# Score matmuls of two or four heads tied together in one two-bank PSUM tile, in a two-layer hybrid decoder trunk

## The chip, the cores and the metric

The kernel runs on one core of one Trainium2 chip. The metric is the device time of one execution in microseconds (us), the median of several runs. The engines are PE (TensorE: matmuls, with PEld for the loading of their stationary operands), DVE (VectorE), ACT (ScalarE), POOL (GpSimd) and SP, which issues most DMAs. PSUM, where matmuls write, has eight banks of 512 fp32 columns.

## The reference, cut to what matters

Two layers over 512 positions of width 1024, in fp32. Layer 0 (mLSTM and pooling) is untouched by the change. Layer 1 is a sparse attention with 16 heads of 64 columns and an indexer of 4 heads of 64 columns that picks keys:

```python
score = jnp.einsum('bqh,bqhs->bqs', wib, jax.nn.relu(jnp.einsum('bqhd,bsd->bqhs', qib, ki)))
score = jnp.where((key_pos[None, :] <= t[:, None])[None], score, -jnp.inf)
_, idx = lax.top_k(score, top_k)
...
logits = jnp.einsum('bqhd,bqkhd->bqhk', qb, ksel).astype(jnp.float32) * (C_HEAD_DIM ** -0.5)
logits = logits + bias.transpose(0, 1, 3, 2)
logits = jnp.where(valid[:, :, None, :], logits, -jnp.inf)
probs = jax.nn.softmax(logits, axis=-1).astype(v.dtype)
return jnp.einsum('bqhk,bqkhd->bqhd', probs, vsel)
```

## The kernel before, in words

Every fp32 operand is split into a high and a low half, and each product is three matmuls (high by high, high by low, low by high).

Layer 1 works in blocks of 128 queries (i = 0 to 3), with n = 128 (i + 1) keys, and in four groups c of four heads. `scores(i)` (called for i = 1, 2, 3) makes the indexer's scores, `select(i, part)` marks the largest of them by rounds of MAX8 and MATCH_REPLACE on DVE, and `attend(c, i)` does one block of queries for four heads, two pairs of heads one after the other. A pair is: score matmuls into PSUM (`qk`), bias and mask added on the way out of PSUM by DVE (L808, which also gives the row's extreme), exp on ACT (L810), reciprocal on DVE (L811), scaling on ACT (L812), transposes on PE (L820, into `tr`), their split on ACT and DVE (`pt_h`, `pt_l`), nine or so matmuls with the values (L829 to L831, into `po`), and a product with the gate on DVE (L835). The bias tile `cb` that L808 reads is made by POOL (L805) in one of two buffers.

A head has 64 columns, so a score matmul contracts over 64 rows only. Two heads of a pair lie in rows 0 to 63 and 64 to 127 of the same tiles. `head_pair` writes its six matmuls (three products of two heads) in turn, e = 0 and e = 1, into two separate banks:

```python
p = [bank("qk"), bank("qk")]
for j in range(3):
    for e in range(2):
```

`qk` is a pool of two buffers of one bank each, so a pair takes both, and each bank is free for the next pair once its own head has been read out. The projections around (`q_proj`, `k_proj`, `v_proj`, `z_proj`, `ckv_proj`; matmuls at L182 to L184 and L198 to L200 into `mm`) run over all this time and fill PE between the steps of the attention.

`ORDER` gives the order in which the steps are written, but the order on each engine is made when the kernel is built: a list scheduler takes the instructions by their priority as soon as, by its own reckoning, their inputs and buffers are free. So the six matmuls of a pair need not stand side by side on PE. There are 228 score matmuls, all at L669: 108 over 256 columns (keys), 60 over 384 and 60 over 512.

The last step, the output projection, uses `dense_ch4` twice (hf = 0, 1): four accumulators each, two from `mm` and two from `qk`, read out by `store` (L848).

Of the kernel before, what the change touches and what calls it, by code (L numbers as in the profile page):

```python
# [2 lines left out]

# [5 lines left out]
F32 = mybir.dt.float32  # L9
# [49 lines left out]
def trunk(ctx: ExitStack, tc: tile.TileContext, a: dict, out: bass.AP):  # L59
    nc = tc.nc  # L60
    V, A, G, T = nc.vector, nc.scalar, nc.gpsimd, nc.tensor
# [5 lines left out]
    ps = {}  # L67
    ps_pools = ExitStack()

    def psum_pools(**banks):  # L70
        ps_pools.close()
        ps.clear()
        for n, b in banks.items():
            ps[n] = ps_pools.enter_context(tc.tile_pool(name="ps_" + n, bufs=b, space=PSUM))
# [4 lines left out]
    def bank(n):  # L79
        return ps[n].tile([128, 512], F32, name=n)  # L80

    def mm():
        return bank("mm")
# [31 lines left out]
    def split(h, l, src):  # L115
        A.copy(h, src)  # L116
        sub_f32r(l, src, h)
# [17 lines left out]
    def wtile(shape, loads, queue=nc.sync):  # L135
        n = math.prod(shape)
        raw = wp.tile([128, 1024], F32, name="raw", bufs=3)
        wh = wp.tile([128, 1024], F32R, name="wh")
        wl = wp.tile([128, 1024], F32R, name="wl")

        def view(t):
            t = t[:, :n]
            if len(shape) == 2:
                t = t.rearrange("p (x y) -> p x y", x=shape[0])
            return t
        for sl, src in loads:
            queue.dma_start(view(raw)[:, sl[0], sl[1]], src)
        A.copy(wh[:, :n], raw[:, :n])  # L148
        low_engine[0].tensor_tensor(wl[:, :n], raw[:, :n], wh[:, :n].bitcast(F32), op=ALU.subtract)  # L149
        return view(wh), view(wl)  # L150
# [3 lines left out]
    def wrows(w, r0, nk, c0, n):  # L154
        return w[r0:r0 + 128 * nk, c0:c0 + n].rearrange("(k p) c -> p k c", p=128)
# [38 lines left out]
    def part_ch(act, w, ks, ps):  # L194
        wh, wl = w
        for j, k in enumerate(ks):
            ah, al = act(k)
            T.matmul(ps, wh[:, j], ah, start=(k == 0), stop=False)  # L198
            T.matmul(ps, wh[:, j], al, start=False, stop=False)  # L199
            T.matmul(ps, wl[:, j], ah, start=False, stop=(k == NK - 1))  # L200

    def dense_ch4(act, w, hf, evac, alloc):

        acc = [alloc(c) for c in range(4)]
        for k0 in range(0, NK, 2):
            wh, wl = wtile([2, 512], [((ALL, ALL), wrows(w, 128 * k0, 2, 512 * hf, 512))])
            for c in range(4):
                cs = slice(128 * c, 128 * c + 128)
                part_ch(act, (wh[:, :, cs], wl[:, :, cs]), (k0, k0 + 1), acc[c])
                if k0 == NK - 2:  # L210
                    evac(4 * hf + c, acc[c])
# [8 lines left out]
    xn = lambda k: (xn_h[:, k], xn_l[:, k])  # L220
# [105 lines left out]
    w_in, w_out = a["e_w_in"], a["e_w_out"]  # L326


    with ExitStack() as l0:
# [141 lines left out]
        with ExitStack() as la:  # L471
            p0 = la.enter_context(tc.tile_pool(name="p0a", bufs=1))
# [134 lines left out]

    w_in, w_out = a["o_w_in"], a["o_w_out"]
    w_uk, w_uv = a["o_w_uk"], a["o_w_uv"]
    psum_pools(mm=2, bg=1, qk=2, tr=2, po=1)  # L610
    GR = ((0, 1), (2, 3))
    p2 = ctx.enter_context(tc.tile_pool(name="p2", bufs=1))
    zy = p2.tile([128, 8, S], F32, name="zy")
# [8 lines left out]
    qi_h, qi_l = (p1.tile([128, 2, S], F32R, name=n, tag=n, bufs=2) for n in ("aq_h", "aq_l"))  # L622
    ki_h, ki_l = (p2.tile([128, S], F32R, name=n, tag=n, bufs=3) for n in ("ak_h", "ak_l"))
# [36 lines left out]
    def ckv_proj():  # L660
        dense_tok(xn, range(NK), [(w_in, 1024, 256)], ev_ckv, GR)

    def head_pair(q, k, n):

        p = [bank("qk"), bank("qk")]
        for j in range(3):
            for e in range(2):
                es = slice(64 * e, 64 * e + 64)
                T.matmul(p[e][:, :n], q(es, j), k(es, j), start=(j == 0), stop=(j == 2))  # L669
        return p  # L670

    near = {0: tmask}
    far = {}
# [2 lines left out]
    def scores(i):  # L676
        n = 128 * (i + 1)
        qs = slice(128 * i, 128 * i + 128)
        acc = sel[i] = (p2 if i == 3 else p1).tile([128, n], F32, name=f"sel{i}")
        G.memset(acc[:, :n - 128], 0.0)  # L680
        G.tensor_copy(acc[:, n - 128:], tmask)
        pair = {}
        for h in range(4):
            if h % 2 == 0:
                pair = head_pair(lambda e, j: (qi_h, qi_h, qi_l)[j][e, h // 2, qs],
                                 lambda e, j: (ki_h, ki_l, ki_h)[j][e, :n], n)
            p = pair[h % 2]
            rl = t1.tile([128, 512], F32, name="relu", tag="cb")
            A.activation(rl[:, :n], p[:, :n], AF.Relu)
            V.scalar_tensor_tensor(acc, rl[:, :n], wi[:, i, h:h + 1], acc, op0=ALU.mult, op1=ALU.add)  # L690
# [93 lines left out]
    def attend(c, i):  # L784
        (q_h, q_l), (k_h, k_l), (v_h, v_l) = Q[c]["q"], Q[c]["k"], Q[c]["v"]
        bias = Q[c]["bias"]
        n = 128 * (i + 1)
        nn = max(n, 256)
        qs = slice(128 * i, 128 * i + 128)
        lo = max(n - 256, 0)  # L790
        for pr in range(2):
            probs = []
            pq = head_pair(lambda e, j: (q_h, q_h, q_l)[j][e, pr, qs], lambda e, j: (k_h, k_l, k_h)[j][e, pr, :nn], nn)
            for e in range(2):
                hd = 2 * pr + e
                p = pq[e]
                if i == 3:
                    cb = sel[i][e]
                else:
                    cb = t1.tile([128, 384], F32, name="cb", tag="cb")  # L800
                    if lo:
                        G.tensor_copy(cb[:, :lo], far[i])
                rev = bias[:, hd, n - lo - 1:n - lo]
                rev = bass.AP(tensor=rev.tensor, offset=rev.offset, ap=[rev.ap[0], [-1, n - lo]])
                G.tensor_tensor(cb[:, lo:n], near[i], rev, op=ALU.add)  # L805
                lg = p2.tile([128, 512], F32, name="lg", tag="lg", bufs=6)
                st = t1.tile([128, 4], F32, name="st", bufs=4)
                V.tensor_tensor_reduce(out=lg[:, :n], in0=p[:, :n], in1=cb[:, :n], scale=-1.0, scalar=3e38,  # L808
                                       op0=ALU.add, op1=ALU.min, accum_out=st[:, 0:1])
                A.activation(lg[:, :n], lg[:, :n], AF.Exp, scale=-1.0, bias=st[:, 0:1], accum_out=st[:, 1:2])  # L810
                V.reciprocal(st[:, 2:3], st[:, 1:2])  # L811
                A.activation(lg[:, :n], lg[:, :n], AF.Copy, scale=st[:, 2:3])  # L812
                probs.append(lg)
            po = bank("po")
            for s0 in range(0, i + 1, 2):
                ss = range(s0, min(s0 + 2, i + 1))
                p = bank("tr")
                for s in ss:
                    for e in range(2):
                        T.transpose(p[:, 256 * (s - s0) + 128 * e:256 * (s - s0) + 128 * e + 128],  # L820
                                    probs[e][:, 128 * s:128 * s + 128], ident)
                m = 256 * len(ss)
                pt_h = p2.tile([128, 512], F32R, name="pt_h", bufs=2)
                pt_l = p2.tile([128, 512], F32R, name="pt_l", bufs=2)
                split(pt_h[:, :m], pt_l[:, :m], p[:, :m])
                for s in ss:
                    cs = slice(128 * pr, 128 * pr + 128)
                    ps = slice(256 * (s - s0), 256 * (s - s0) + 256)
                    T.matmul(po[:, :256], v_h[:, s, cs], pt_h[:, ps], start=(s == 0), stop=False)  # L829
                    T.matmul(po[:, :256], v_l[:, s, cs], pt_h[:, ps], start=False, stop=False)  # L830
                    T.matmul(po[:, :256], v_h[:, s, cs], pt_l[:, ps], start=False, stop=(s == i))  # L831
            for e in range(2):
                es = slice(64 * e, 64 * e + 64)
                y = zy[es, 2 * c + pr, qs]
                V.tensor_tensor(y, po[es, 128 * e:128 * e + 128], y, op=ALU.mult)  # L835

    def y_split(c, i=None):

        cs, qs = slice(2 * c, 2 * c + 2), ALL if i is None else slice(128 * i, 128 * i + 128)
        split(xn_h[:, cs, qs], xn_l[:, cs, qs], zy[:, cs, qs])  # L840

    step = dict(i=scores, c=ckv_proj, q=q_proj, k=k_proj, v=v_proj, z=z_proj, s=select, a=attend, y=y_split)
    run(ORDER, **step)

# [4 lines left out]
        nc.scalar.dma_start(out[128 * c:128 * c + 128], o)  # L849

    for hf in range(2):
        dense_ch4(xn, w_out, hf, store, lambda c: bank(("mm", "qk", "mm", "qk")[c]))


def layout(inputs):
# [34 lines left out]
```

## Time and profile before

| | us |
|---|---|
| three runs, median (lowest to highest) | 774.74 (774.5 to 776.12) |
| the profiled execution, device time | 773.58 |
| its span, first to last instruction | 771.8 |
| PE busy in the span | 751.6 (97%) |
| DVE busy | 464.8 (60%) |
| ACT busy | 398.1 (52%) |
| POOL busy | 304.7 (39%) |
| score matmuls (L669), first to last start | 488.8 to 723.8 |

The profiled execution took 1.8 us more than its span, and lies 1.2 us under the median. Busy time of PE is counted from overlapping matmuls (each starts before the one ahead has drained), so it says that PE had something in it, not that it worked at its peak. What a matmul costs the stream is read from one start to the next.

### The profile page before, as it was taken

Reading aid. Unit: us, or ns where it says so; the run is one execution under the profiler, and the core shown is the slowest. Engines: PE = TensorE matmul, PEld = TensorE weight load, DVE = VectorE, ACT = ScalarE, POOL = GpSimd, SP = SyncE. Lnnn points to the kernel's source line nnn. Section 1 sums busy time; section 2 is a strip of 40 time slices with the busy share of each in tenths; the row PEclk is TensorE's granted clock in tenths of the full one; section 3 lists DMA queues with packets and bytes.
Section 4 is the critical chain, followed back from the end, with each engine's and each line's share of the span. In section 5 each row is a group of like instructions: output and inputs, shape, how many; then the busy total and the mean of one; then the engine's idle time right before and its main releaser. Section 6 shows DMA issues by size and latency. Waiting matters only on the chain.

```text
span 771.8 us, 11177 instructions
## 1 busy us (share of the span) xinstructions
PE 751.6 (97%) x4123; PEld 631.6 (82%) x4123; DVE 464.8 (60%) x988; ACT 398.1 (52%) x778; POOL 304.7 (39%) x246
## 2 busy tenths in 40 slices
PE   7989999999999999999999999998999999999988
PEld 5887888887888889888888888987788888887766
DVE  6686534344727765147224572599999978877531
ACT  6445333282445543355433353545667688887620
POOL 5545448732003020131363393445124555472241
PEclk9999999999999999999999999999999999999999
DMA  7523342345332313332322244422321221020051
GB/s 222 155 75 84 84 108 74 105 122 150 106 86 69 87 63 110 82 96 87 89 84 61 88 154 123 111 69 69 82 69 42 69 69 55 9 91 13 28 192 54
DMA packets 83990, 69.20 MB, mean 90 GB/s; under 512 B 3884, under 2 KB 71900, under 8 KB 83936
## 3 DMA queue, kind: packets, MB, share of 16 engines
q1 hardware_dynamic: 82144, 65.83, 29.6%
q10 hardware_dynamic: 1760, 2.66, 1.0%
q8 instruction: 32, 0.52, 0.3%
q14 instruction: 22, 0.18, 0.1%
q0 software_dynamic: 32, 0.01, 0.0%
HBM read 64.25 MB, written 4.23 MB: 89 GB/s over the span
## 4 chain that ended last, share of the span: by engine, by line
PE 84%; DVE 9%; ACT 2%; DMA 2%; issue 2%; POOL 1%; SPq 1%; DVEq 0%; ACTq 0%; POOLq 0%
PE mm L198 13%; PE mm L199 13%; PE mm L200 12%; PE mm L182 8%; PE mm L183 8%; PE mm L184 8%; PE qk L669 5%; PE tr L820 2%; PE po L829 2%; PE po L831 2%; DVE sel L698 1%; DVE m L697 1%; DMA raw<-in_e_w_in_dram 1%; PE po L830 1%; DVE wl L149 1%
## 5 line engine op out<-in xcount | busy, mean ns | idle before, releaser
L149 POOL TENSOR_TENSOR wl<-raw,wh 128x1024 fp32r<-128x1024 f32 (+4 forms) x65 | 148.7, 2290 | 274.4 <-ACT wh L148 230.6
L148 ACT CAST wh<-raw 128x1024 fp32r<-128x1024 f32 (+4 forms) x117 | 113.4, 971 | 172.8 <-PE mm L199 52.3
L198 PE MATMUL mm<-xn_h,wh 128*128 128x512 f32 x336 | 132.8, 397 | 3.1 <-DVE v_l L363 2.0
L200 PE MATMUL mm<-xn_h,wl 128*128 128x512 f32 x336 | 132.6, 395 | 0.0
L199 PE MATMUL mm<-xn_l,wh 128*128 128x512 f32 x336 | 132.3, 394 | 0.0
L183 PE MATMUL mm<-wl,xn_h 128*128 128x256 f32 (+2 forms) x384 | 123.9, 323 | 0.0
L184 PE MATMUL mm<-wh,xn_l 128*128 128x256 f32 (+2 forms) x384 | 123.2, 322 | 0.0
L182 PE MATMUL mm<-wh,xn_h 128*128 128x256 f32 (+2 forms) x384 | 121.6, 325 | 1.0 <-DVE xT L595 0.9
L149 DVE TENSOR_TENSOR wl<-raw,wh 128x1024 fp32r<-128x1024 f32 (+2 forms) x52 | 66.0, 1269 | 63.2 <-ACT wh L148 62.7
L182 PEld LDWEIGHTS mm<-wh,xn_h 128*128 128x128 f32 x384 | 72.0, 189 | 9.2 <-ACT wh L148 1.3
L183 PEld LDWEIGHTS mm<-wl,xn_h 128*128 128x128 f32 x384 | 72.3, 188 | 7.0 <-issue 1.1
L184 PEld LDWEIGHTS mm<-wh,xn_l 128*128 128x128 f32 x384 | 72.2, 188 | 6.7 <-issue 0.7
L198 PEld LDWEIGHTS mm<-xn_h,wh 128*128 128x128 f32 x336 | 63.2, 189 | 17.1 <-DVE v_l L363 2.1
L199 PEld LDWEIGHTS mm<-xn_l,wh 128*128 128x128 f32 x336 | 63.3, 188 | 14.5 <-issue 0.6
L200 PEld LDWEIGHTS mm<-xn_h,wl 128*128 128x128 f32 x336 | 63.3, 188 | 13.8
L200 PE MATMUL mm<-y_h,wl 128*128 128x512 f32 x128 | 50.1, 393 | 0.6 <-DVE wl L149 0.6
L199 PE MATMUL mm<-y_l,wh 128*128 128x512 f32 x128 | 50.4, 394 | 0.0
L198 PE MATMUL mm<-y_h,wh 128*128 128x512 f32 x128 | 48.9, 395 | 0.9 <-ACT y_h L116 0.9
L504 DVE SCALAR_TENSOR_TENSOR cv<-mm,s_conv,cv 128x511 f32<-128x511 f32 (+2 forms) x48 | 35.9, 747 | 16.3 <-ACT cv L502 15.3
L810 ACT ACTIVATE lg<-lg,st 128x128 f32<-128x128 f32 (+3 forms) x64 | 35.8, 561 | 6.1 <-DVE st L808 5.9
L812 ACT ACTIVATE lg<-lg,st 128x128 f32<-128x128 f32 (+3 forms) x64 | 34.0, 557 | 7.4 <-DVE st L811 7.4
L805 POOL TENSOR_TENSOR cb<-sel,abias 128x256 f32<-128x256 f32 x32 | 24.5, 770 | 30.1 <-DVE st L808 22.1
(272 smaller groups left out, 1578.0 us busy)
## 6 DMA issues: line engine op xcount, KB each, us to landing
raw<-in_e_w_in_dram SPq DMA_DIRECT2D x52, 512.0 KB, 3.8
raw<-in_o_w_in_dram SPq DMA_DIRECT2D x18, 512.0 KB, 3.9
raw<-in_e_w_out_dram SPq DMA_DIRECT2D x16, 512.0 KB, 3.8
raw<-in_o_w_out_dram SPq DMA_DIRECT2D x8, 512.0 KB, 3.6
xT<-in_xT_dram SPq DMA_DIRECT2D x8, 256.0 KB, 4.2
x_one<-xT SPq DMA_DIRECT2D x8, 256.0 KB, 3.0
abias<-lines SPq DMA_DIRECT2D x4, 512.0 KB, 4.2
o_sb<-x_one SPq DMA_DIRECT2D x8, 256.0 KB, 4.4
```

What stands on the lines that cost most here:

```text
L148: A.copy(wh[:, :n], raw[:, :n])
L149: low_engine[0].tensor_tensor(wl[:, :n], raw[:, :n], wh[:, :n].bitcast(F32), op=ALU.subtract)
L182: T.matmul(acc[t][:, :n], ah[:, ts], wh[:, j], start=first, stop=False)
L183: T.matmul(acc[t][:, :n], ah[:, ts], wl[:, j], start=False, stop=False)
L184: T.matmul(acc[t][:, :n], al[:, ts], wh[:, j], start=False, stop=last)
L198: T.matmul(ps, wh[:, j], ah, start=(k == 0), stop=False)
L199: T.matmul(ps, wh[:, j], al, start=False, stop=False)
L200: T.matmul(ps, wl[:, j], ah, start=False, stop=(k == NK - 1))
L504: V.scalar_tensor_tensor(u[:, j:], ps[:, :S - j], w[:, 3 - j:4 - j], u[:, j:], op0=ALU.mult, op1=ALU.add)
L669: T.matmul(p[e][:, :n], q(es, j), k(es, j), start=(j == 0), stop=(j == 2))
L810: A.activation(lg[:, :n], lg[:, :n], AF.Exp, scale=-1.0, bias=st[:, 0:1], accum_out=st[:, 1:2])
L812: A.activation(lg[:, :n], lg[:, :n], AF.Copy, scale=st[:, 2:3])
```

## The change

`head_pairs` takes one tile of two banks from `qk`, whose pool now has one such buffer (the same two banks). Head e = 0 writes the first bank and e = 1 the second. Where the keys are at most 256 columns, both pairs of the four heads share the tile (256 columns each in either bank) and their 12 matmuls are issued as one sequence; above, each pair has its 6. `together` gives every matmul after the first of a sequence a high priority and makes it depend on the one ahead (an order on the engine, no semaphore), so that they come out side by side. The output projection takes its two `qk` accumulators from one such tile.

```diff
-    psum_pools(mm=2, bg=1, qk=2, tr=2, po=1)
+    psum_pools(mm=2, bg=1, qk=1, tr=2, po=1)
...
-    def head_pair(q, k, n):
-
-        p = [bank("qk"), bank("qk")]
-        for j in range(3):
-            for e in range(2):
-                es = slice(64 * e, 64 * e + 64)
-                T.matmul(p[e][:, :n], q(es, j), k(es, j), start=(j == 0), stop=(j == 2))
-        return p
+    def together(steps):
+
+        last = steps[0]()
+        for step in steps[1:]:
+            with tc.high_priority():
+                ins = step()
+            tc.add_manual_dep(ins.ins, last.ins.name, mybir.DependencyInfo(
+                mybir.DependencyClass.NoSync, mybir.DependencyReason.DATA), reason="together")
+            last = ins
+
+    def head_pairs(q, k, n):
+
+
+
+        for p0 in (0,) if n <= 256 else (0, 1):
+            two = ps["qk"].tile([128, 2, 512], F32, name="qk")
+            prs = (0, 1) if n <= 256 else (p0,)
+            p = [two[:, :, 256 * (pr - p0):256 * (pr - p0) + n] for pr in prs]
+            rows = (slice(0, 64), slice(64, 128))
+            together([partial(T.matmul, dst[:, e], q(es, j, pr), k(es, j, pr), start=(j == 0), stop=(j == 2))
+                      for pr, dst in zip(prs, p) for j in range(3) for e, es in enumerate(rows)])
+            yield from p
...
-        for pr in range(2):
+        pairs = head_pairs(lambda e, j, pr: (q_h, q_h, q_l)[j][e, pr, qs],
+                           lambda e, j, pr: (k_h, k_l, k_h)[j][e, pr, :nn], nn)
+        for pr, pq in enumerate(pairs):
             probs = []
-            pq = head_pair(lambda e, j: (q_h, q_h, q_l)[j][e, pr, qs], lambda e, j: (k_h, k_l, k_h)[j][e, pr, :nn], nn)
...
-                p = pq[e]
+                p = pq[:, e]
...
     for hf in range(2):
-        dense_ch4(xn, w_out, hf, store, lambda c: bank(("mm", "qk", "mm", "qk")[c]))
+        two = ps["qk"].tile([128, 2, 512], F32, name="qk")
+        dense_ch4(xn, w_out, hf, store, lambda c: two[:, c // 2] if c % 2 else mm())
```

How PE's order changes, at three places. A row is a line of the kernel, the operation, what it writes and reads, and the size of the output; lines of the changed kernel are later by one to 16 (L183 there is L182 here, L836 is L820).

PE before, at an `attend` of a block with 384 keys (`ak`, `aq` are the keys and queries of one group of heads, high and low):

```order
L183 MATMUL mm<-wl,xn_h 128x256
L669 MATMUL qk<-ak_h,aq_h 128x384
L669 MATMUL qk<-ak_l,aq_h 128x384
L669 MATMUL qk<-ak_h,aq_l 128x384
L182 MATMUL mm<-wh,xn_h 128x256
L183 MATMUL mm<-wl,xn_h 128x256
L669 MATMUL qk<-ak_h,aq_h 128x384
L669 MATMUL qk<-ak_l,aq_h 128x384
L669 MATMUL qk<-ak_h,aq_l 128x384
L829 MATMUL po<-pt_h,av_h 128x256
```

PE now, at an `attend` of a block with 384 keys:

```order
L185 MATMUL mm<-wh,ckv_l 128x256
L666 MATMUL qk<-ak_h,aq_h 128x384
L669 MATMUL qk<-ak_h,aq_h 128x384
L669 MATMUL qk<-ak_l,aq_h 128x384 x2
L669 MATMUL qk<-ak_h,aq_l 128x384 x2
L183 MATMUL mm<-wh,xn_h 128x256
```

The three matmuls of one head and the three of the other stood apart, with projection matmuls between them; now the six stand together, head beside head.

PE before, at the first `attend` with 256 keys: one pair's last transposes, and the halves of a pair on either side of one of them.

```order
L184 MATMUL mm<-wh,ckv_l 128x256
L820 MATMUL tr<-cst,lg 128x128 x2
L669 MATMUL qk<-ak_h,aq_h 128x256
L669 MATMUL qk<-ak_l,aq_h 128x256
L669 MATMUL qk<-ak_h,aq_l 128x256
L820 MATMUL tr<-cst,lg 128x128
L669 MATMUL qk<-ak_h,aq_h 128x256
L669 MATMUL qk<-ak_l,aq_h 128x256
L669 MATMUL qk<-ak_h,aq_l 128x256
L182 MATMUL mm<-wh,ckv_h 128x256
```

PE now, at the second sequence of four heads:

```order
L185 MATMUL mm<-wh,ckv_l 128x256
L836 MATMUL tr<-cst,lg 128x128
L666 MATMUL qk<-ak_h,aq_h 128x256
L669 MATMUL qk<-ak_h,aq_h 128x256
L669 MATMUL qk<-ak_l,aq_h 128x256 x2
L669 MATMUL qk<-ak_h,aq_l 128x256 x2
L669 MATMUL qk<-ak_h,aq_h 128x256 x2
L669 MATMUL qk<-ak_l,aq_h 128x256 x2
L669 MATMUL qk<-ak_h,aq_l 128x256 x2
L199 MATMUL mm<-xn_h,wh 128x512
```

Twelve matmuls of four heads now stand in one piece, right behind the first transpose of the four heads ahead of them.

DVE now, at the first four heads (L824 is L808, the read-out of one head; L712 and L713 are the rounds of `select`, L114 and L762 read out the projections):

```order
L824 ISA lg,st<-qk,cb 128x128
L824 ISA st 128x1
L824 ISA lg,st<-qk,cb 128x128
L824 ISA st 128x1
L762 SCALAR_TENSOR_TENSOR ak_l<-bg,s_gk,ak_h 128x2x256
L114 TENSOR_TENSOR av_l<-mm,av_h 128x256
L712 MAX m_5341<-sel_4434 128x8
L827 RECIPROCAL st<-st 128x1
L824 ISA lg,st<-qk,cb 128x128
L824 ISA st 128x1
L827 RECIPROCAL st<-st 128x1
L824 ISA lg,st<-qk,cb 128x128
```

The order on DVE is much as it was (before, the same four read-outs stood with two L113, one L747 and two rows of `select` among them), but PE's next score matmul now has to wait for the last row shown, where it waited for the first.

Over the whole program the score matmuls stood in 65 uninterrupted runs on PE before, and stand in 30 now: 9 of twelve matmuls at 256 columns, 10 of six at 384, and at 512 9 of six, one of four and one of two. No engine has an instruction more or less. The order of the other work on PE, DVE, ACT and POOL changes with it from the first score matmul on.

## Rows read from the trace of the kernel before

**Rows 1.** The page: busy time by engine, and the chain that ended last, by engine.

```profile
PE 751.6 (97%) x4123; PEld 631.6 (82%) x4123; DVE 464.8 (60%) x988; ACT 398.1 (52%) x778; POOL 304.7 (39%) x246
...
PE 84%; DVE 9%; ACT 2%; DMA 2%; issue 2%; POOL 1%; SPq 1%; DVEq 0%; ACTq 0%; POOLq 0%
```

**Rows 2.** Stages: length, busy PE, PEld, DVE, ACT, POOL, granted PE clock, DMA share, GB/s.

```profile
480.00:545.00 65.00, 62.98 (x416) 55.56 (x415) 53.03 (x137) 33.68 (x76) 28.27 (x19) 0.97 0.28 75
545.00:620.00 75.00, 73.72 (x488) 63.75 (x487) 73.20 (x207) 51.94 (x120) 30.15 (x37) 1.00 0.24 67
620.00:724.00 104.00, 103.47 (x693) 84.94 (x692) 80.42 (x260) 87.35 (x212) 51.17 (x62) 1.00 0.13 44
724.00:772.00 48.00, 41.19 (x193) 33.56 (x192) 12.51 (x32) 10.07 (x21) 12.04 (x5) 1.00 0.32 110
```

**Rows 3.** Line L669, one of three products: shortest, median, longest ns, first to last start.

```profile
L669 PE MATMUL qk<-ak_h,aq_h x76: 380/437/502, 488.8 to 723.8; 64*128 64x256 f32 x36, 64*128 64x384 f32 x20, 64*128 64x512 f32 x20
```

**Rows 4.** PE in order of time, a whole pair at 256 columns: start, us, what.

```profile
488.61 0.28 PE L184 MATMUL mm<-wh,xn_l 128*128 128x256 f32 x1
488.81 0.39 PE L669 MATMUL qk<-ak_h,aq_h 64*128 64x256 f32 x2
489.04 0.28 PE L669 MATMUL qk<-ak_l,aq_h 64*128 64x256 f32 x2
489.15 0.28 PE L669 MATMUL qk<-ak_h,aq_l 64*128 64x256 f32 x2
489.36 0.38 PE L182 MATMUL mm<-wh,xn_h 128*128 128x256 f32 x1
489.58 0.28 PE L183 MATMUL mm<-wl,xn_h 128*128 128x256 f32 x1
489.70 0.29 PE L184 MATMUL mm<-wh,xn_l 128*128 128x256 f32 x1
```

**Rows 5.** PE in order of time, one head alone at 256 columns.

```profile
569.67 0.29 PE L184 MATMUL mm<-wh,ckv_l 128*128 128x256 f32 x1
569.89 0.38 PE L669 MATMUL qk<-ak_h,aq_h 64*128 64x256 f32 x1
570.11 0.28 PE L669 MATMUL qk<-ak_l,aq_h 64*128 64x256 f32 x1
570.23 0.28 PE L669 MATMUL qk<-ak_h,aq_l 64*128 64x256 f32 x1
570.44 0.39 PE L182 MATMUL mm<-wh,xn_h 128*128 128x256 f32 x1
570.67 0.28 PE L183 MATMUL mm<-wl,xn_h 128*128 128x256 f32 x1
```

**Rows 6.** PE, before and after three matmuls of one head at 384 columns.

```profile
619.41 0.28 PE L183 MATMUL mm<-wl,xn_h 128*128 128x256 f32 x1
...
620.56 0.28 PE L183 MATMUL mm<-wl,xn_h 128*128 128x256 f32 x1
```

**Rows 7.** PE, before and after three matmuls of one head at 512 columns.

```profile
649.43 0.28 PE L183 MATMUL mm<-wl,xn_h 128*128 128x256 f32 x1
...
650.75 0.28 PE L182 MATMUL mm<-wh,xn_h 128*128 128x256 f32 x1
```

**Rows 8.** What PE waited for from 480 on: total us, times, longest us.

```profile
PE mm L182 <- DVE av_l L113: 3.2, 3, 2.0
```

**Rows 9.** Two stretches around a wait of PE, columns as in the stages.

```profile
526.00:529.10 3.10, 1.10 (x8) 0.50 (x6) 3.10 (x8) 1.91 (x5) 0.00 (x0) 1.00 0.65 169
529.10:533.40 4.30, 4.28 (x21) 3.98 (x22) 4.27 (x10) 2.73 (x6) 2.32 (x2) 0.62 0.00 0
```

**Rows 10.** Read-outs of one head by DVE (ns), and POOL's bias tile.

```profile
L808 DVE CUSTOM_DVE_ANT_0 lg<-qk,cb x48: 273/422/559, 549.4 to 724.7; 128x128 f32<-128x128 f32 x16, 128x256 f32<-128x256 f32 x16, 128x384 f32<-128x384 f32 x16
L808 DVE CUSTOM_DVE_ANT_0 lg<-qk,sel x8: 680/686/692, 625.6 to 698.8; 128x512 f32<-128x512 f32 x8
...
L805 POOL TENSOR_TENSOR cb<-sel,abias 128x256 f32<-128x256 f32 x32 | 24.5, 770 | 30.1 <-DVE st L808 22.1
```

More of the change, by code (lines that the diff above doesn't have):

```diff
@@ L2 @@
 from contextlib import ExitStack
+from functools import partial
 import concourse.bass as bass
@@ L681, in scores @@
         G.tensor_copy(acc[:, n - 128:], tmask)
-        pair = {}
+        pairs = head_pairs(lambda e, j, pr: (qi_h, qi_h, qi_l)[j][e, pr, qs],
+                           lambda e, j, pr: (ki_h, ki_l, ki_h)[j][e, :n], n)
         for h in range(4):
             if h % 2 == 0:
-                pair = head_pair(lambda e, j: (qi_h, qi_h, qi_l)[j][e, h // 2, qs],
-                                 lambda e, j: (ki_h, ki_l, ki_h)[j][e, :n], n)
-            p = pair[h % 2]
+                pair = next(pairs)
+            p = pair[:, h % 2]
             rl = t1.tile([128, 512], F32, name="relu", tag="cb")
```

## The prediction

> **What bounds the kernel now.** I read the page first: PE is busy 97% of the span and carries 84% of the chain that ended last [rows 1]. That is an average, so next the stages from 480 us on, where layer 1's attention lies [rows 2]. From 480 to 545 DVE, in the rounds of the selection, is busy for 53.0 of 65 us, and PE stands still for 2.0. From 545 to 620 PE has 73.7 of 75 us and DVE 73.2: both are full. From 620 to 724 PE has 103.5 of 104, while DVE has 80.4 and ACT 87.4. After 724 no score matmul is left. So PE time taken out is worth most after 620, little between 545 and 620, next to nothing ahead of that. The waits of PE agree: the largest entry is for DVE, 3.2 us in three waits [rows 8].
>
> The score matmuls start from 488.8 to 723.8 [rows 3]. What they cost PE's stream is read in order of time, from one start to the next. Ordinary matmuls of 256 columns start 0.12 us apart (489.58 to 489.70 [rows 4]).
>
> **What a run of score matmuls costs.** A "run" is what stands uninterrupted between other matmuls. From the last ordinary matmul before a run to the second one after it I take the difference of the starts, less two ordinary steps of 0.12. A whole pair at 256 columns, six matmuls: 489.58 - 488.61 = 0.97, less 0.24 = 0.73 us [rows 4]. One head alone, three matmuls: 570.67 - 569.67 = 1.00, less 0.24 = 0.76 us [rows 5]. The reader should stop here: half the work costs the same. Two things make it so. In a pair the two heads are in PE side by side ("x2" rows with three distinct starts for six matmuls). And a run has a fixed price: the first score matmul starts 0.20 to 0.22 after the one ahead, the second 0.22 to 0.23 after the first, the third only 0.11, the first ordinary one 0.21 later, and the next again 0.22. Three steps of 0.115 are 0.35, so 0.40 us is fixed.
>
> One head alone at 384 columns: 1.15 - 0.24 = 0.91 [rows 6]; at 512: 1.32 - 0.24 = 1.08 [rows 7]. Steps of 0.17 and 0.23 leave the same 0.40.
>
> The Trainium skill states such a price: "TensorEngine Tiling (Array Packing)", Key Properties, says that changing the tiling mode, not merely the tile, drains TensorE. It gives no duration; the rows above agree with it, and by the rule too every run pays once, so that the sum by it is the sum by the rows below.
>
> **PE's sum.** Before: 65 runs with, counted by distinct starts in the trace, 82 steps at 256 columns, 46 at 384 and 45 at 512: 65 x 0.40 + 82 x 0.115 + 46 x 0.17 + 45 x 0.23 = 26.0 + 9.4 + 7.8 + 10.4 = 53.6 us. After, from the 30 runs of the new order: 12.0 + 54 x 0.115 + 30 x 0.17 + 30 x 0.23 = 12.0 + 6.2 + 5.1 + 6.9 = 30.2 us. PE is spared 23.4 us. No trace row shows a run of twelve. If the step from one pair to the next inside it cost the extra 0.11 of a run's second step, that is 9 x 0.11 = 1.0 us less; at best nothing. I take nothing, since the third step inside a run is an ordinary one. The same count by stages (runs by their place in the trace) gives 1.0 us before 545, 5.9 from 545 to 620, and 16.9 from 620 to 724 (0.4 above the total, since one of the new runs is split in two).
>
> **What of it reaches the end.**
> 1. Before 545: 1.0 us, behind DVE's selection. Bounds 0 and 1; I take 0.
> 2. 545 to 620: DVE has 73.2 of 75 us, so at most 1.8 of the 5.9 can come here, unless DVE's work drifts later. I take 1.
> 3. 620 to 724: PE would need 103.5 - 16.9 = 86.6 us. ACT needs 87.4 and DVE 80.4, so the stage can't fall below 87.4: at most 16.6. Three engines would then be near full in one loop (score, read-out, exp, reciprocal, scaling, transpose, split, values). The nearest row for two engines full at once is the stage 545 to 620, at 98% each; three in a loop will do less. With ACT at 95% the stage takes 92 us, a gain of 12; at 90%, 97 and a gain of 7; at 99%, 16.
> 4. The new wait. PE's next score run now needs the whole tile read out, where it needed one head's bank. Queued behind it on PE are transposes and value matmuls, for which ACT and DVE wait in turn. A read-out of one head takes 0.27 to 0.69 us on DVE [rows 10]; before, PE had no listed wait on a score bank. Bounds: nothing, since other PE work stands between runs, and one more read-out of about 0.5 us at each of the 28 boundaries, 14 us. The trace is nearer to the lower end; I take 1.
> 5. The clock. After the 2.0 us wait at 527 to 529, in which PE was busy for 1.1 of 3.1 us, the granted clock of the next 4.3 us is 0.62, a mix of 2.4 and 1.2 GHz [rows 9]; that cost some 4.3 x 0.38 = 1.6 us. PE arrives earlier at the same DVE rows, so waits of this kind may come more often: nothing to three more, 0 to 5 us. I take none, as the waits that DVE causes are already in points 2 and 3.
> 6. The output projection waits for two accumulators to be read out together instead of one at a time. In the stage after 724 PE is busy for 41.2 of 48 us, and the next accumulators in `mm` cover a read-out. Nothing; 0.7 us if the cover fails.
>
> Sum: 0 + 1 + 12 - 1 = 12 us. Against the profiled execution, 773.58 - 12 = 761.6; the median of the runs is 1.2 above it, which gives 762.7. I forecast 762.5.
>
> **Rivals.**
> A, PE's gain comes nearly whole. DVE's total from 545 to 724 is 73.2 + 80.4 = 153.6 us in 179; if its work spreads, the two stages could shrink by up to 22 us with DVE at 98%. For it: PE and DVE both held 98% for 75 us already. Against it: the reading-out is in bursts and ACT is needed too. Time: 775 - 22 = 753.
>
> B, DVE and ACT keep most of it. PE runs into unread tiles and unfinished probabilities, and only a third of point 3 is left after the waits, with a clock drop or two: 4 to 6 us, about 769.5. For it: DVE has 98% from 545 to 620, and PE meets the same DVE rows with 7 us less work behind it. Against it: 104 us follow in which DVE idled for 24. The Trainium skill puts this rival as a rule: "TensorEngine Tiling (Array Packing)", PSUM Bottleneck, says that tiling speeds up TensorE but not the reading-out of PSUM, which may become the bottleneck. The stages' rows agree for 545 to 620 and not for what follows.
>
> C, slower. One tile is all the score space there is, and a run of four heads holds it until four heads are read, each needing a bias tile of 0.77 us from POOL in two buffers [rows 10]: some 4 x 0.77 = 3.1 us; a pair at 384 or 512 columns holds it for two read-outs, up to 1.4. Over 9 and 20 runs that is 28 + 28 = 56 us. All of it hidden costs nothing; it decides against the change when more than the 13 us that points 1 to 3 give, about a quarter, stand on PE. At 40%, 22 us, the time is 784; just past the point, 780. Against it: projections, transposes and value matmuls stand between almost all runs.
>
> D, no change: what PE saves returns as waits in the same stages, or heads that stand apart are cheaper than rows 5 to 7 say. Time 774.5. Against the second: three widths give the same fixed price.
>
> **How the numbers follow.** The forecast, 757 to 767: 0.50. A, 749 to 757: 0.17. B, 767 to 773: 0.22. D, within 0.2% (1.5 us, about what a measurement of this kernel can tell from no change): 0.05. C: 0.06. The forecast's own range is that of ACT at 90 to 99% in point 3. The range for 8 in 10 runs from 751 (A's middle cut) to 771 (most of B), leaving out C, D and the outer ends of A and B. Faster is the forecast with A and B, 0.89; same 0.05; slower 0.06.
>
> **What would show it.** In the new profile score matmuls should come as "x2" rows in runs of three or six steps; the price of a run by the same differences should be 0.75, 0.91 and 1.08, and about 1.1 for twelve matmuls. The stage up to the same DVE work (the last selection) should end within 2 us of where it did. From there to the last score matmul the stretch should be some 12 us shorter, with DVE and ACT above 85% and PE with 5% of waits where it had 0.5%. Waits of PE for DVE at the first score matmul of a run, above 3 us in total, would be rival C's sign; waits of the transposes on ACT, rival B's. The forecast is wrong if score runs cost less than thought before (then PE busy falls by less than 20 us) or if DVE's selection, moved in its queue, ends later than before.

## The result and the profile after

The changed kernel takes 764.8 us (median of 4 runs, 762.97 to 766.08), beside 775.36 for the kernel before on the same chip: a ratio of 0.986 with an interval of 0.984 to 0.989. The forecast was 762.5. The profiled execution took 762.97 us with a span of 761.2, which is 10.6 less than the span before; the accounts below are made in that span, of one execution of each kernel.

The page after, busy time by engine and the chain that ended last, by engine (line numbers have moved: L808, L829 and L835 of before are L824, L845 and L851 now, L182 and L198 are L183 and L199):

```profile
PE 733.4 (96%) x4123; PEld 622.7 (82%) x4123; DVE 465.4 (61%) x988; ACT 396.4 (52%) x778; POOL 306.4 (40%) x246
...
PE 76%; DVE 11%; ACT 7%; issue 2%; DMA 1%; POOL 1%; SPq 1%; DVEq 0%; ACTq 0%; POOLq 0%
```

Against [rows 1], PE has 18.2 us less to do with the same 4123 matmuls, and its share of the chain falls from 84% to 76%: ACT and DVE now end last in places where PE did.

PE after, in order of time (start, us, what), around a run of twelve score matmuls:

```profile
487.62 0.28 PE L184 MATMUL mm<-wl,xn_h 128*128 128x256 f32 x1
487.74 0.28 PE L185 MATMUL mm<-wh,xn_l 128*128 128x256 f32 x1
487.94 0.38 PE L666 MATMUL qk<-ak_h,aq_h 64*128 64x256 f32 x1
487.95 0.38 PE L669 MATMUL qk<-ak_h,aq_h 64*128 64x256 f32 x1
488.17 0.28 PE L669 MATMUL qk<-ak_l,aq_h 64*128 64x256 f32 x2
488.29 0.28 PE L669 MATMUL qk<-ak_h,aq_l 64*128 64x256 f32 x2
488.40 0.28 PE L669 MATMUL qk<-ak_h,aq_h 64*128 64x256 f32 x2
488.52 0.28 PE L669 MATMUL qk<-ak_l,aq_h 64*128 64x256 f32 x2
488.64 0.28 PE L669 MATMUL qk<-ak_h,aq_l 64*128 64x256 f32 x2
488.85 0.38 PE L183 MATMUL mm<-wh,xn_h 128*128 128x256 f32 x1
489.08 0.28 PE L184 MATMUL mm<-wl,xn_h 128*128 128x256 f32 x1
```

By the prediction's own way of pricing a run: 489.08 - 487.74 = 1.34, less two ordinary steps of 0.12, is 1.10 us for four heads. Before, 0.73 us bought two heads [rows 4] and 0.76 one [rows 5]. The second pair comes in at ordinary steps (488.29 to 488.40), so there is one entry and one exit for all four. Summed over all runs, from the starts in both traces and with PE's waits inside them left out, score work costs 55.4 us of PE's stream in 65 runs before, and 31.8 in 30 runs after: 23.6 us are spared. This is an estimate, good to some 0.6 us, since it turns on what is taken for an ordinary step beside a run.

Stages after, columns as in [rows 2]:

```profile
480.00:545.00 65.00, 60.99 (x405) 54.41 (x404) 57.74 (x155) 33.36 (x75) 28.61 (x19) 0.95 0.27 74
545.00:620.00 75.00, 72.51 (x508) 63.59 (x507) 70.56 (x204) 55.76 (x133) 34.05 (x39) 1.00 0.24 68
620.00:724.00 104.00, 98.98 (x743) 86.38 (x742) 82.60 (x259) 88.67 (x216) 54.58 (x62) 1.00 0.17 54
```

Length less PE's busy time is PE's idle time. In these three stages it was 2.0 + 1.3 + 0.5 = 3.8 us [rows 2]; it is 4.0 + 2.5 + 5.0 = 11.5 now: 7.7 us of what was spared have turned into waits. What PE waited for after 480 (total us, times, longest us):

```profile
PE mm L183 <- DVE av_l L114: 5.0, 4, 3.4
PE po L845 <- DVE zy L851: 3.3, 4, 1.5
PE qk L666 <- DVE st L824: 1.8, 4, 0.6
PE mm L199 <- ACT xn_h L117: 1.1, 1, 1.1
PE po L847 <- DVE pt_l L114: 1.1, 2, 0.7
```

The third row is the new wait, for the whole score tile to be read: 1.8 us. The wait for `av_l`, whose longest was 2.0 us [rows 8], now reaches 3.4.

Fixed stages of time compare unlike work once the kernels have drifted apart. So the same stretches between marks in the work: first score matmul, first score matmul of the 25th head block of 76, last head block, and 0.1 us behind the start of the last value matmul of attention. Windows after, same columns:

```profile
487.90:602.20 114.30, 108.42 (x702) 94.57 (x700) 109.36 (x297) 67.16 (x149) 47.63 (x42) 0.97 0.24 67
602.20:708.70 106.50, 102.14 (x804) 90.11 (x805) 91.01 (x287) 95.27 (x237) 60.31 (x73) 1.00 0.17 53
708.70:726.80 18.10, 15.17 (x92) 12.77 (x88) 9.37 (x33) 10.68 (x28) 8.21 (x5) 1.00 0.29 94
```

And the same marks before, which were not shown yet:

```profile
488.80:603.20 114.40, 111.10 (x703) 95.45 (x702) 106.28 (x284) 67.80 (x149) 45.59 (x40) 0.99 0.24 67
603.20:723.80 120.60, 120.07 (x820) 99.93 (x819) 96.78 (x313) 99.44 (x246) 61.40 (x76) 1.00 0.15 47
723.80:738.90 15.10, 13.46 (x74) 11.27 (x73) 6.17 (x21) 7.76 (x20) 6.09 (x4) 1.00 0.25 81
```

This is the account of the result. The scores begin 0.9 us earlier. The first stretch, with the same 702 or 703 matmuls, gains 0.1. The second gains 14.1. The third loses 3.0: it holds 18 matmuls more, which came from the second (1.7 us of PE's busy time), and 1.3 us more idle time. From its end to the end of the span it was 771.8 - 738.9 = 32.9 us, and is 34.4: 1.5 lost. 0.9 + 0.1 + 14.1 - 3.0 - 1.5 = 10.6.

The last loss, and part of the first stretch's, is PE's clock. From the third stretch to the end of the span, before and after:

```profile
738.90:771.80 32.90, 27.93 (x122) 22.49 (x120) 6.54 (x11) 2.51 (x3) 5.96 (x3) 1.00 0.36 123
726.80:761.20 34.40, 29.41 (x122) 23.56 (x120) 6.54 (x11) 2.50 (x3) 4.80 (x2) 0.95 0.30 104
```

The same 122 matmuls, at a clock of 0.95 where it was 1.00; PE is idle for 4.99 us of it, and was for 4.97. Windows after, around the two places where the clock fell (behind the length: busy time by engine, then the clock):

```profile
526.00:529.10 3.10, 0.55 (x4) 0.55 (x5) 3.10 (x8) 0.00 (x0) 0.84 (x2) 1.00 0.65 167
529.10:533.40 4.30, 3.74 (x21) 3.45 (x20) 4.20 (x14) 2.77 (x6) 2.39 (x1) 0.60 0.00 0
533.40:537.00 3.60, 3.60 (x15) 3.17 (x14) 2.72 (x11) 2.03 (x6) 2.51 (x2) 0.53 0.56 146
724.00:728.00 4.00, 1.33 (x6) 0.90 (x6) 2.78 (x8) 0.81 (x3) 1.47 (x1) 0.99 0.77 225
728.00:732.00 4.00, 3.90 (x11) 3.10 (x12) 0.69 (x2) 0.05 (x1) 0.00 (x0) 0.58 0.47 172
```

PE was busy for 0.55 of the 3.10 us ahead of the first fall and for 1.33 of the 4.00 ahead of the second; the clock behind (0.60, 0.53 and 0.58) is a mix of 2.4 and 1.2 GHz. I estimate the price as length times what the clock lacks: 4.3 x 0.40 + 3.6 x 0.47 = 3.4 us at 530, and 4.0 x 0.42 = 1.7 at 728, together 5.1. In the profiled execution of before there was only the first from 480 us on, of 1.6 us [rows 9].

### The profile page after: what moved, and what is told of

The parts are those of the page before. It is cut to its first block, busy times and chain, and to the rows that moved or that the text cites. A ratio compares the mean times of both kernels' runs of the same rounds, so it can differ in the third digit from the quotient of the medians.

```text
span 761.2 us, 11155 instructions
## 1 busy us (share of the span) xinstructions
PE 733.4 (96%) x4123; PEld 622.7 (82%) x4123; DVE 465.4 (61%) x988; ACT 396.4 (52%) x778; POOL 306.4 (40%) x246
## 4 chain that ended last, share of the span: by engine, by line
PE 76%; DVE 11%; ACT 7%; issue 2%; DMA 1%; POOL 1%; SPq 1%; DVEq 0%; ACTq 0%; POOLq 0%
PE mm L199 13%; PE mm L200 13%; PE mm L201 13%; PE mm L183 7%; PE mm L184 7%; PE mm L185 7%; DVE sel L713 2%; ACT lg L826 2%; DVE wl L150 2%; DVE m L712 1%; PE tr L836 1%; ACT wh L149 1%; DVE sel L705 1%; PE qk L199 1%; PE qk L200 1%
## 5 line engine op out<-in xcount | busy, mean ns | idle before, releaser
L150 POOL TENSOR_TENSOR wl<-raw,wh 128x1024 fp32r<-128x1024 f32 (+4 forms) x65 | 149.9, 2307 | 277.6 <-ACT wh L149 234.1
L199 PE MATMUL mm<-xn_h,wh 128*128 128x512 f32 x336 | 134.0, 400 | 3.0 <-DVE v_l L364 1.9
L183 PE MATMUL mm<-wh,xn_h 128*128 128x256 f32 (+2 forms) x384 | 121.4, 325 | 1.0 <-DVE xT L596 0.9
L150 DVE TENSOR_TENSOR wl<-raw,wh 128x1024 fp32r<-128x1024 f32 (+2 forms) x52 | 65.6, 1262 | 62.4 <-ACT wh L149 62.0
L183 PEld LDWEIGHTS mm<-wh,xn_h 128*128 128x128 f32 x384 | 71.8, 188 | 9.3 <-ACT wh L149 1.3
L199 PEld LDWEIGHTS mm<-xn_h,wh 128*128 128x128 f32 x336 | 63.7, 190 | 17.7 <-DVE v_l L364 2.0
L199 PE MATMUL mm<-y_h,wh 128*128 128x512 f32 x128 | 49.0, 396 | 0.9 <-ACT y_h L117 0.9
L126 POOL TENSOR_TENSOR q_r<-q_ss,mhalf 128x8 f32<-128x8 f32 x16 | 28.2, 1760 | 22.9 <-DVE q_ss L123 21.2
```

Source lines behind the costliest of these rows:

```text
L126: G.tensor_tensor(dst, ss, mhalf[:, :n], op=ALU.pow)
L183: T.matmul(acc[t][:, :n], ah[:, ts], wh[:, j], start=first, stop=False)
```

## The experiments

Twelve kernels, each timed beside the kernel before. For those that change how the scores are issued, "spared" is score work on PE against before, "idle" and "clock" what the trace shows more of idle PE time from 470 us on and of time lost there to the lower clock, all in us, estimated from the trace of one execution each; "left" is spared less idle less clock.

| kernel | score runs | ratio (95%) | spared | idle | clock | left | span gained |
|---|---|---|---|---|---|---|---|
| the change | 30 | 0.9862 (0.9837 to 0.9888) | 23.6 | 7.7 | 3.4 | 12.5 | 10.6 |
| tied only | 53 | 0.9957 (0.9939 to 0.9974) | 9.6 | 5.1 | 1.7 | 2.8 | 1.5 |
| no fours | 39 | 0.9896 (0.9878 to 0.9914) | 19.0 | 8.9 | 1.7 | 8.4 | 6.4 |
| not tied | 39 | 0.9857 (0.9840 to 0.9873) | 18.7 | 5.5 | 3.4 | 9.8 | 8.9 |
| head by head | 30 | 0.9843 (0.9822 to 0.9865) | 23.4 | 6.8 | 3.4 | 13.2 | 11.9 |

In every row "left" is above the measured gain of the span, by 0.9 to 2.0 us.

**Tied only.** The kernel before, with a pair's six matmuls tied together as in the change, but the two one-bank tiles kept.

```diff
-        for j in range(3):
-            for e in range(2):
...
+        together([partial(T.matmul, p[e][:, :n], q(es, j), k(es, j), start=(j == 0), stop=(j == 2))
+                  for j in range(3) for e, es in enumerate(rows)])
```

> The kernel before with its two one-bank score buffers, the six matmuls of a pair tied together, nothing else. The build leaves 53 runs of score matmuls on PE (many pairs as one and five), where before has 65 and the changed kernel 30. Theory (the price is 0.40 us a run plus the steps): PE's score time 42 us, 12 less than before; as in the changed kernel some 45% of it reaches the end: 5 us, a ratio to before of 0.9935. Rival (the tying does it, the tile is a detail): ratio 0.986, as the changed kernel. Rival (the single tile does harm that the tying pays for): ratio under 0.984.

772.4 us, against 775.8: a third of the gain, and less than the 5 us of the theory. Tying alone leaves 53 runs.

**No fours.** The changed kernel, with pairs at 256 columns too.

```diff
-        for p0 in (0,) if n <= 256 else (0, 1):
+        for p0 in (0, 1):
...
-            prs = (0, 1) if n <= 256 else (p0,)
+            prs = (p0,)
```

> The changed kernel with a tile for each pair at 256 columns too, so 39 runs of score matmuls and none of twelve. Theory (price of a run): 9 x 0.40 = 3.6 us more PE time than the changed kernel, of which 1.6 to 3.6 us reach the end: 766.5 to 768.5, ratio to before 0.988 to 0.991. Rival (four heads hold the tile too long, and PE waits for their read-out): faster than the changed kernel by 1 us or more, ratio 0.984 or less.

767.4 us. Nine runs more take 4.6 us of PE's stream (23.6 less 19.0), where 9 x 0.40 is 3.6, and 2.6 us of the median; its interval and that of the change just overlap (0.9878 and 0.9888).

**Not tied.** The changed kernel, with the matmuls issued in turn, without raised priority or added dependence.

```diff
-        last = steps[0]()
-        for step in steps[1:]:
...
+        for step in steps:
+            step()
```

> The changed kernel with its shared tiles, but without the priority and the order that tie the matmuls. The build leaves 39 runs, all pairs at 384 and 512 columns whole and only the fours at 256 in pieces. Theory (one tile makes both heads' bank free at the same time, and that alone brings a pair together): like the kernel without fours, ratio 0.988 to 0.991. Rival (the tying is what brings the gain): ratio 0.995 or more.

764.8 us, the same as the changed kernel, at a ratio below the 0.988 to 0.991 that the theory gave. The trace has 39 runs instead of 30, so 4.9 us less is spared, but there are 2.2 us less of new idle time; the times can't be told apart. The kernel without fours has 39 runs too and is 2.7 us slower, with the intervals apart: what differs in the table is the idle time, 8.9 us against 5.5. So the number of runs sets what PE is spared, not what reaches the end. Together with the first experiment: the shared tile, which comes free in one piece, does the work of keeping the pairs together, and the tying adds nothing that these runs could measure.

**Head by head.** The changed kernel, with the three matmuls of a head issued in sequence, and then those of the head in the other half of the rows.

```diff
-                      for pr, dst in zip(prs, p) for j in range(3) for e, es in enumerate(rows)])
+                      for pr, dst in zip(prs, p) for e, es in enumerate(rows) for j in range(3)])
```

> The changed kernel with the three matmuls of one head ahead of the three of the other in each pair, still tied. Theory (PE runs the two row halves at the same time as long as both stand in its queue, whichever comes first; three pairs before stood so and started 10 ns apart): six matmuls still in three distinct starts, the time of the changed kernel within 1.5 us. Rival (only neighbours run at the same time): a run of six in six steps, 18 us more PE time, 773 us or more, no faster than before.

764.0 us, the same. PE of this kernel in order of time, a run of twelve:

```profile
487.26 0.38 PE L666 MATMUL qk<-ak_h,aq_h 64*128 64x256 f32 x1
487.27 0.38 PE L669 MATMUL qk<-ak_h,aq_h 64*128 64x256 f32 x1
487.49 0.29 PE L669 MATMUL qk<-ak_l,aq_h 64*128 64x256 f32 x2
```

The second head's first matmul, now fourth in the queue, still starts 0.01 us after the first head's: the two halves of the rows are worked on side by side whether their matmuls alternate or not.

**Less work on DVE.** Two edits, each to both kernels, that take load off DVE, which the prediction named as the limit from 545 to 620. First, the low halves of six weight groups are split off on POOL (lower-case letters in the order string).

```diff
-ORDER = ("C q0 i1 i2 z0 v0 i3 s10 k0 z2 s11 v1 Z1 K1 Q1 s12 s20 s21 s22 a00 s13 Z3 s30 s23 s31 K2 s32 a01 "
+ORDER = ("c q0 i1 i2 z0 v0 i3 s10 k0 z2 s11 v1 z1 k1 q1 s12 s20 s21 s22 a00 s13 z3 s30 s23 s31 k2 s32 a01 "
```

> The changed kernel with the low halves of the weights of seven steps (C, Z1, K1, Q1, Z3, K2 of the order, where a capital letter gives them to DVE) made by POOL instead. That takes some 14 tiles of about 1.1 us off DVE between 490 and 600 us, where POOL is busy less than half of the time. Theory (part of the gain stays behind DVE, which is full there): PE's 3.4 us wait near 528 and the low clock after it shrink, 3 to 8 us faster than the changed kernel, 757 to 762. Rival (the waits come from the chain from engine to engine, not from DVE's load): no gain or slower, since POOL takes 2.3 us for a tile that DVE makes in 1.1.

> The kernel before with the same letters. Theory: it waited less for DVE (6.8 us of PE waits after 470, against 14.5), so it gains less than the changed kernel does, 0 to 4 us: 771 to 775.5. Rival: the letters help both alike, or neither.

The gain of 3 to 8 us that was expected of the changed kernel did not come: it rises to 772.0 us (0.9948, 0.9935 to 0.9961), the kernel before to 782.1 (1.0083, 1.0066 to 1.0099): 6 to 7 us each. The difference between them stays at 10. DVE is lighter in that stage (61.2 us of 75, against 70.56), POOL heavier (45.3 against 34.05), and POOL takes longer for such a split (in the page after, means of 2307 ns on POOL and 1262 on DVE, over mixed sizes), so the edit also puts slower work into the weights' path and tells little by itself. The second edit only removes: two rounds of `select` instead of four, so that 64 keys are marked instead of 128, and half of the selection is left out.

```diff
-        for _ in range(4):
+        for _ in range(2):
```

> The changed kernel with two instead of four rounds in each part of the selection (it marks 64 keys, not 128): 48 of the 96 selection operations, some 26 us, are taken off DVE. To be set against the next. Theory (DVE's load holds back what PE saves): PE's waits after 470 fall from 14.5 to under 8 us, and the distance to the kernel before with the same cut is 75% or more of the PE time between them.

> The kernel before with the same half selection. With DVE freer its score banks come free earlier, and the build leaves 55 runs of score matmuls, not 65: about 48 us of PE time for scores against 32.5 in the changed kernel with half the selection, 15.5 apart. Theory: 75% or more of that, 12 to 15 us, is the difference of the two times. Rival (chains and the clock hold it back, not DVE's load): 45% as in the full kernels, 7 us.

The changed kernel stays at 765.0 us (0.9865, 0.9848 to 0.9882), the kernel before falls to 772.0 (0.9949, 0.9930 to 0.9967): the two are 7 us apart, as the rival said, and not 12 to 15. Stage 545 to 620 of the changed kernel with half the selection, and its two largest waits:

```profile
545.00:620.00 75.00, 72.09 (x514) 63.87 (x513) 52.41 (x163) 58.73 (x141) 34.09 (x41) 1.00 0.24 68
```

```profile
PE po L845 <- DVE zy L851: 5.6, 6, 1.5
PE mm L183 <- DVE av_l L114: 4.2, 4, 2.4
```

DVE has 18.2 us less in this stage (70.56 to 52.41), and PE does no more in it (72.51 to 72.09). The waits do not go; they come at other places, above all where the one `po` buffer has to be read out before the next head's values. My theory that DVE's load keeps the rest of the gain has fallen. One part of it stands, though. From the first score matmul to that of the 25th head block, this kernel's window is:

```profile
487.60:596.50 108.90, 103.19 (x688) 90.14 (x687) 86.18 (x224) 66.59 (x147) 46.87 (x43) 1.00 0.26 70
```

That is 5.4 us less than in the changed kernel. By estimate 2.2 of them are 14 matmuls put off to later (at 108.42 / 702 = 0.154 us each), and 3 are the clock, 1.00 where it was 0.97; PE's idle time is 5.71 where it was 5.88. The lower clock came back later: the mean over the whole span is 0.990, and was 0.991.

**Another buffer.** All eight PSUM banks are in use, so a second `po` buffer or a third `mm` buffer had to take one of the two of the transposes; the third kernel only gives that one up.

```diff
-    psum_pools(mm=2, bg=1, qk=1, tr=2, po=1)
+    psum_pools(mm=2, bg=1, qk=1, tr=1, po=2)
...
+    psum_pools(mm=3, bg=1, qk=1, tr=1, po=1)
...
+    psum_pools(mm=2, bg=1, qk=1, tr=1, po=1)
```

> The changed kernel with one buffer moved from the transposes (tr) to the value matmuls (po): tr 1, po 2. New theory, since half a selection freed DVE and freed nothing for the changed kernel: what holds back the rest of the gain is PE's order against buffers of which there are one or two, whose read-out takes a chain through ACT and DVE. The waits of po for zy (3.3 us in the changed kernel) should go, the time fall by 2 to 4 us against the kernel with tr 1 alone. Rival (any wait removed comes back at the next link): the waits move to tr and pt_l and the time stays.

> The changed kernel with one buffer moved from tr to the projections (mm): tr 1, mm 3. Theory: the waits of mm for av_l (5.0 us, and the low clock after the longest) should go, and the time fall by 3 to 6 us against tr 1 alone. Rival as for two po.

> The control: the changed kernel with tr 1 and that bank unused. Both theories: slower than the changed kernel by 1 to 6 us, since transposes then wait for the split of those ahead.

807.1, 807.9 and 807.5 us (1.0395, 1.0425 and 1.0381 of before, the intervals 0.006 to 0.009 wide): all three 42 to 43 us slower than the changed kernel, where 1 to 6 was expected of the third, and not told apart. What PE waited for in the third:

```profile
PE po L845 <- ACT pt_h L117: 18.6, 26, 1.2
```

With one transpose buffer the value matmuls wait for the head's own probabilities, 26 times, a wait that the changed kernel's list does not have. The mean clock of its profiled execution is 0.975 over 805.3 us, where the changed kernel's is 0.991 over 761.2: priced as above, 20.1 against 6.9 us, so that 13 of the 43 us are the clock. That hides whatever a second `po` or a third `mm` buffer is worth. Which buffer holds the rest stays open.

**Filling the tail.** The changed kernel, with nine bf16 matmuls of 512 columns on zeros tied behind the values of the last `attend`. Nobody reads their result.

```diff
+            if (c, i) == (3, 0):
+                pw = bank("bg")
+                together([lambda: end] + [partial(T.matmul, pw, warm2[:, 0:128], warm2, start=True, stop=True)
+                                          for _ in range((5, 4)[pr])])
```

> The changed kernel with nine matmuls on zeros (bf16, 128x512, nobody reads them) put on PE behind the value matmuls of the last attend, where PE waits for 0.56, 1.46 and 1.1 us and its clock is then 0.5 for 3.4 us. Theory (the waits at the end cost a low clock too): the granted clock stays at 1 there, and the end comes about 1.7 us earlier, 763. Rival (the fillers stand in the way of the chain, or the clock costs nothing there): 764.5 to 767.

761.8 us, 0.9819 (0.9792 to 0.9846): 3 us below the changed kernel, with intervals that just overlap; the span is 2.0 shorter. Its windows at the tail:

```profile
724.00:728.00 4.00, 3.32 (x16) 1.66 (x16) 2.73 (x8) 0.40 (x1) 0.98 (x1) 1.00 0.75 260
728.00:732.00 4.00, 4.00 (x19) 3.30 (x18) 1.41 (x3) 0.00 (x0) 0.00 (x0) 1.00 0.52 193
```

PE is busy for 3.32 us of the four where it was for 1.33, and the clock of the next four is 1.00 where it was 0.58, with 19 matmuls in them instead of 11. From 0.1 us behind the start of the last value matmul to the end:

```profile
726.30:759.20 32.90, 28.82 (x126) 22.77 (x124) 6.54 (x11) 2.50 (x3) 4.80 (x2) 0.99 0.31 108
```

That is 32.9 us, as in the kernel before, where the changed kernel takes 34.4. So the 1.5 us lost at the tail are shown to be the clock, and the fillers give them back; the mean clocks agree (0.993 to 0.997 in five executions, where the changed kernel's four have 0.988 to 0.991). The rest of the 2.0 us of the span is not theirs: the scores begin 0.5 us later, and the first stretch is 1.0 us shorter (113.3), where the lower clock near 530 lasted half as long, although nothing was changed there. What part of the 3 us between the medians is of that kind stays open. This is the fastest kernel of the study.

## Why the prediction came out right, point by point

**The price of a run** was right: 1.10 us for twelve matmuls where about 1.1 was said, and 23.6 us spared where the sum gave 23.4. The experiments with 53, 39 and 30 runs spare 9.6, 19 and 23.5. The drain that the Trainium skill states for a change of tiling mode ("TensorEngine Tiling (Array Packing)", Key Properties) agrees with this: each run that disappears spares 0.67 to 0.80 us, of which 0.40 is the fixed price and the rest the steps that heads now share. No run here tells a drain from another fixed cost of going to 64 rows and back.

**PE busy** fell by 18.2 us, less than the 20 that I had named as a sign against me. The sign was badly chosen: a matmul at the lower clock is busy for longer (the first of the output projection, now and before, with the wait ahead of it in brackets), and by estimate 3.4 us more of that make it 21.6.

```profile
728.10 0.79 PE L199 MATMUL mm<-xn_h,wh 128*128 128x512 f32 x1 [1.12 <-ACT xn_h L117]
740.20 0.50 PE L198 MATMUL mm<-xn_h,wh 128*128 128x512 f32 x1 [1.12 <-ACT xn_h L116]
```

**Points 1 and 2** (0 and 1 us up to 620): from the start to the 25th head block 0.9 + 0.1 = 1.0 us were gained. The number is right and its reason is not, which makes the number luck. I argued that DVE, 98% full, lets no more pass; with 18 us of DVE's work gone from the stage PE is idle as long in this stretch, and the kernel is no faster. What stands in the rows is 2.6 us more of PE's idle time (114.30 - 108.42 against 114.40 - 111.10) and 1.8 us more lost to the clock, from a wait for `av_l` that grew from 2.0 to 3.4 us. The rest of what was spared there I can't place. Nor did the last selection stay within 2 us of where it was: it ended at 615.8 before and at 600.4 now.

**Point 3** (12 us): the second stretch gave 14.1, of which 1.7 is work put off to the third: 12.4. DVE was busy for 91.01 of 106.50 us (85%), ACT for 95.27 (89%), and PE idle for 4.1%, where 85% and 5% were said. That ACT sets the floor was an argument; ACT was at 89%, not 95, and no run took load from it. By the prediction's own sum ACT at 90% stood for a gain of 7 us, so the 12 came out near the mark in part by luck. What the rows show is that PE is still the fullest engine, busy for 95.9% of the stretch.

**Point 4** (1 us for the new wait): 1.8 us by the waits of PE itself. The 1.3 us more of idle time in the third stretch are not of this kind: PE's listed waits there are all for `zy`. Rival C's sign, above 3 us, did not come. The waits of the transposes on ACT, rival B's sign, were 0.3 us.

**Point 5** (no clock) is, in the profiled executions, the step that failed: 5.1 us where 1.6 was, so 3.5 lost. The bounds of 0 to 5 held it. I had named the wait at 527 to 529 as the place for it, and still took none, as the waits were in points 2 and 3 already. But a wait and the lower clock behind it are two prices: filling the tail gave back 1.5 us by the clock alone. How much of this holds for the medians is open. The mean clock of a kernel differs from one execution to the next: in the 38 executions of the kernel before that were timed beside the experiments it was 0.988 to 0.998, the middle one 0.991, and the profiled one had 0.996; the changed kernel's four had 0.988 to 0.991. Between the middle ones, 0.991 and 0.990, the clock costs by estimate some 0.7 us more (0.010 x 763 against 0.009 x 774), not 3.5.

**Point 6**: nothing beyond the clock stands behind the last value matmul (1.5 lost, the clock's price is 1.7, PE's idle time is 4.99 and was 4.97), so the projection waits no more than before.

The sum was 12 and the span gave 10.6. The median then lies 2.3 us above the forecast: 1.4 by the sum, and most of the rest because the medians are 1.8 us above the profiled executions, before and after, where 1.2 was reckoned. The rule that reading-out may become the bottleneck (the Trainium skill, "TensorEngine Tiling (Array Packing)", PSUM Bottleneck) has one part shown, 1.8 us of waits for the score tile. That the other idle time comes from the order in which PE waits for one head's chain after another is argued, not shown: it is there with DVE full and with DVE light.

## What to carry to other kernels

Where 64-row matmuls stand among 128-row ones, count the uninterrupted runs, not the matmuls: the cost of a run is read from starts, and a shared tile that comes free in one piece was enough here to bring most of them together (39 runs without any tie, where 65 were). Where PE is at 97%, don't count on all that it is spared: of 23.6 us here 10.6 came through, and the rest surfaced as waits of up to 3.4 us and, in the profiled execution, as the lower clock behind them. What the clock took at the tail, 1.5 us, nine matmuls on zeros gave back.

## What I had not expected of the hardware

Issue order within a run of score matmuls did not matter here: three matmuls of one half of the rows ahead of three of the other start 0.01 us apart all the same.

The clock differs between executions that have much the same waits. At its tail PE waits three times in the kernel before (0.34, 1.30 and 1.12 us) and in the changed one (0.56, 1.46 and 1.12), behind the same two tiles, and in its profiled execution the kernel before did not lose the clock. Windows of before there:

```profile
736.00:740.00 4.00, 1.44 (x7) 0.90 (x6) 2.88 (x8) 1.13 (x4) 4.00 (x2) 1.00 0.85 265
740.00:744.00 4.00, 3.80 (x17) 3.14 (x18) 1.40 (x3) 0.14 (x1) 0.05 (x1) 1.00 0.71 265
```

PE was busy for 1.44 of 4 us, then at 1.00; after the change for 1.33, then at 0.58. That is one execution of each kernel, and the mean clock of one kernel differs from execution to execution by more than the 0.002 of the span that this fall costs (0.988 to 0.998 before), so these rows don't show that the change itself made the difference at the tail.

One transpose buffer fewer costs 43 us, four times what the whole change gains; by estimate 13 of them are the clock.
